# Out projection as seven products of quarter sums

## The chip, the cores and the metric

The kernel runs on one core of one Trainium2 chip, in one launch. The metric is the device time of that core in microseconds (us), median of 3 runs, 1201.58 us before the change (1201.33 to 1201.64). Engines are called as the profile calls them: PE (TensorE matmul), PEld (its weight loads), DVE (VectorE), ACT (ScalarE), POOL (GpSimd), SP (SyncE, which issues most DMAs).

## The reference

One layer: row norm, an input projection with pooling and gated linear attention, an out projection, a residual, a second row norm and a squared-ReLU MLP. What matters here is the end of the mixer and what follows it:

```python
def hybrid_mixer(u, ..., w_out):
    ...
    m = jax.nn.sigmoid(ga) * y_a + jax.nn.sigmoid(gb) * y_b
    return jnp.einsum('bld,de->ble', m, w_out)          # (1024 x 1024) x (1024 x 1024)

h = h + hybrid_mixer(rmsnorm(h, norm_mix[l]), ...)
h = h + squared_relu_mlp(rmsnorm(h, norm_ffn[l]), w_ff1[l], w_ff2[l])
return rmsnorm(h, norm_final)[:, N_META:]
```

All is float32. The kernel keeps that precision by splitting each operand into a high part (rounded to the PE format) and a low part (the rest), and forming three products: high x high, high x low, low x high (`mm3`).

## The kernel before

Tokens are taken as 8 tiles of 128, in two halves of 512. Stages in time: row norms and turns of x (0 to 50 us), gates by a seven-product scheme over quarters (`Quarters`, to about 250 us), pooling and attention (to 440), the second half's y_b blocks (`yb_block(n, 1)`, to 488), the out projection (488 to 600), the first MLP product (again `Quarters`, to about 900), the second MLP product.

The order on PE is the order in which the code is written, over the whole kernel. ACT, DVE and POOL are ordered by a scheduler by its own priorities and costs, but within `start` (the first stage) all three are in written order, and around the out projection ACT and DVE are (`in_order`, `any_order`); SP is there too for the loads (`"loads"`). A DMA that POOL issues, or that any engine issues, waits on that engine's queue until what it depends on is done.

In `start`, each row tile is squared on ACT, its scale 1/rms is made from the sum (`first_rms`) by DVE for tiles 0 to 2 and by POOL for tiles 3 to 7 and the meta rows, DVE scales the row (`normed`, L680), and PE turns it. POOL's operations are the L631 to L639 group.

The gated sum m leaves the y_b blocks as high and low parts `MH`, `ML` (per token half; 8 blocks of 128 channels). The out projection `out_tile(t, ch)` makes a product for each of 8 tiles and 2 column halves `ch`, 8 blocks x 3 matmuls each, with weights `wo` rounded by `load_wo` (ACT copy, DVE subtraction). `x_again` puts x into `acc`, and DVE adds the product to it. For `ch` = 1 the row is then complete: it is stored to `h_dram`, normed (`layer_norm`), and two tiles later turned on PE by `turn_tile`, which also forms the MLP's quarter sums.

Of the kernel before, what the change touches and what calls it, by code (L numbers as in the profile page):

```python
# [15 lines left out]
P = 128  # L16
# [99 lines left out]
def kernel(  # L116
# [52 lines left out]
    pm_dram = dp.tile([2, 2, P, 4, HALF], F32, name="pm_dram")  # L169
    hf_dram = [dp.tile([NPAIR, P, HALF], F32, name=f"hf{m}_dram") for m in range(7)]  # L170
# [66 lines left out]
    def layer_norm(xt, u):  # L237

        scaled(xt, u, inv_rms(xt, u))

    def inv_rms(xt, u):
        rows = xt.shape[0]
        ss = ln_stat[ln_n[0] % 4][:rows]
        ln_n[0] += 1
        act.activation(u, xt, ACT.Square, accum_out=ss)
        return inv_sqrt(ss, 1, 1.0 / D)

# [40 lines left out]
    A11, A12, A21, A22, S2, S1, S5, S6, S7 = range(9)  # L288
# [573 lines left out]

    def gate_stage():
# [10 lines left out]
        for _ in S["gate_run"]:  # L874
            pass
# [255 lines left out]
    def early_gates():  # L1131
# [7 lines left out]
        fetch_wo(0, 0, S["raw3"])  # L1139
# [12 lines left out]
    def yb_block(n, h):  # L1152
        j = YB[h][n]

        def fn(*wbs):
# [6 lines left out]
            for e in range(2):  # L1162
# [20 lines left out]
                if h and e and n == 1:  # L1183
                    load_wo(0, 1)()
                if not h:
                    dve.tensor_tensor(gl, b, gl, ALU.mult)
                dve.tensor_tensor(gl, gl, ml, ALU.add)
# [297 lines left out]
    def merge_open():  # L1485
# [4 lines left out]
        S["wo"] = [left.push("wo0", [P, 2, KT, HALF], F32R)]  # L1490
        S["left_acc"] = left.mark()
        S["acc"] = left.push("acc", [P, 8, D], F32)
# [4 lines left out]
        fetch_wo(0, 1, S["acc"][:, 5])  # L1497
# [5 lines left out]
    def x_again(t):  # L1503
        nc.sync.dma_start(S["acc"][:, t], x[t * P : (t + 1) * P, :])

    fetched = {}

    def fetch_wo(ch, kk, at=None):

        c, rows = slice(ch * HALF, (ch + 1) * HALF), w_out[kk * 256 : (kk + 1) * 256]  # L1510
        ap = rows[:, c].rearrange("(k p) c -> p k c", p=P)
        if at is None:
            at = raw.load(ap, D)
        else:
            nc.sync.dma_start(at.rearrange("p (k c) -> p k c", k=2), ap)
        fetched[ch, kk] = at.rearrange("p (k c) -> p k c", k=2)

    def load_wo(ch, kk):
        def fn():
            if (ch, kk) not in fetched:  # L1520
                fetch_wo(ch, kk)
            wo, r = S["wo"][ch][:, :, 2 * kk : 2 * kk + 2], fetched.pop((ch, kk))
            act.activation(wo[:, 0], r, ACT.Copy)
            pending.append(lambda: dve.tensor_tensor(wo[:, 1], r, f32(wo[:, 0]), ALU.subtract))
            if ch:
                late()

        return fn

    step(one, merge_open)  # L1530
    def wo1_open():
        any_order("order")
        raw.back()
        right.pop_to(0)
        buffer("u2", 2, D)
        S["u2p"] = right.push("u2p", [P, 2, HALF], F32)
        S["rawx0"] = right.push("rawx0", [P, D], F32)
        raw.lend(S["rawx0"])
        S["right_ff"] = right.mark()
        S["wo"].append(right.push("wo1", [P, 2, KT, HALF], F32R))  # L1540


    ORDER = (0, 4, 1, 5, 2, 3, 6, 7)

    def out_tile(t, ch):
        def fn():
            half, at = t // 4, (t % 4) * P
            wo = S["wo"][ch]
            b, n = bank("mm"), ORDER.index(t)
            for j in range(2):  # L1550
                if ch and j and n > 1:
                    turn_tile(ORDER[n - 2])
                mm3(
                    b, KT // 2, lambda i: (MH[half][:, 4 * j + i, at : at + P], ML[half][:, 4 * j + i, at : at + P]),
                    lambda i: (wo[:, 0, 4 * j + i], wo[:, 1, 4 * j + i]), first=j == 0, last=j == 1,
                )
            a = S["acc"][:, t, ch * HALF : (ch + 1) * HALF]
# [360 lines left out]
```

## Time and profile before

| | us |
|---|---|
| median of 3 runs | 1201.58 |
| span of the profiled execution (its own time; what lies around it is not in the trace) | 1200.9 |
| PE busy | 1189.0 (99%) |
| DVE busy | 873.0 (73%) |
| ACT busy | 624.7 (52%) |
| POOL busy | 64.8 (5%) |
| PE share of the chain that ended last | 91% |

Busy time of PE counts overlapping matmuls once, so a busy PE says that it never lacked work, and the distance between the starts of two matmuls says what one costs. Idle time on another engine matters only where PE, or the chain, waits for it. A name such as `acc<-b_mm,acc` is output and inputs by the program's names; b_mm, b_x, b_ms are PSUM banks.

### The profile page before, as it was taken

Reading aid. Unit: us, or ns where it says so; the run is one execution under the profiler, and the core shown is the slowest. Engines: PE = TensorE matmul, PEld = TensorE weight load, DVE = VectorE, ACT = ScalarE, POOL = GpSimd, SP = SyncE. Lnnn points to the kernel's source line nnn. Section 1 sums busy time; section 2 is a strip of 40 time slices with the busy share of each in tenths; the row PEclk is TensorE's granted clock in tenths of the full one; section 3 lists DMA queues with packets and bytes.
Section 4 is the critical chain, followed back from the end, with each engine's and each line's share of the span. In section 5 each row is a group of like instructions: output and inputs, shape, how many; then the busy total and the mean of one; then the engine's idle time right before and its main releaser. Section 6 shows DMA issues by size and latency. Waiting matters only on the chain.

```text
span 1200.9 us, 18410 instructions
## 1 busy us (share of the span) xinstructions
PE 1189.0 (99%) x6810; PEld 995.0 (83%) x6810; DVE 873.0 (73%) x1436; ACT 624.7 (52%) x1120; POOL 64.8 (5%) x102
## 2 busy tenths in 40 slices
PE   9999999999999999999999999999999999999997
PEld 8888888898998887888888888888888888888885
DVE  7886677666667888637986767767675887887686
ACT  7677567745446433215654545545454444445554
POOL 2200000000103235000000000000000000000000
PEclk9999999999999999999999999999999999999999
DMA  8243433535107676821264444445389963333532
GB/s 259 36 115 116 126 92 99 156 116 161 50 20 265 196 245 196 323 69 77 88 202 132 158 149 160 148 157 164 125 283 332 330 220 97 97 97 97 167 97 88
DMA packets 143722, 183.29 MB, mean 153 GB/s; under 512 B 10328, under 2 KB 80752, under 8 KB 143120
## 3 DMA queue, kind: packets, MB, share of 16 engines
q1 hardware_dynamic: 141648, 176.55, 45.8%
q0 software_dynamic: 1824, 5.31, 1.5%
q8 instruction: 53, 0.87, 0.3%
q14 instruction: 37, 0.30, 0.1%
q10 hardware_dynamic: 160, 0.27, 0.1%
HBM read 124.41 MB, written 57.67 MB: 152 GB/s over the span
## 4 chain that ended last, share of the span: by engine, by line
PE 91%; DVE 3%; DMA 3%; ACT 1%; issue 1%; SPq 0%; POOL 0%; DVEq 0%; ACTq 0%
PE b_mm L257 10%; PE b_mm L259 10%; PE b_mm L258 10%; PE b_ms L259 10%; PE b_ms L258 10%; PE b_ms L257 10%; PE b_x L257 8%; PE b_x L258 8%; PE b_x L259 8%; PE b_sc L1278 1%; PE b_mx L257 1%; DMA ma_dram<-o 1%; PE b_mx L259 1%; PE b_mx L258 1%; DMA o<-ma_dram 1%; DMA t<-gb_dram 1%
## 5 line engine op out<-in xcount | busy, mean ns | idle before, releaser
L257 PE MATMUL b_mm<-th,w1h 128*128 128x512 f32 (+1 forms) x308 | 115.4, 375 | 0.3 <-DVE c L847 0.3
L259 PE MATMUL b_mm<-th,w1l 128*128 128x512 f32 (+1 forms) x308 | 114.2, 371 | 0.0
L258 PE MATMUL b_mm<-tl,w1h 128*128 128x512 f32 (+1 forms) x308 | 114.1, 371 | 0.0
L257 PE MATMUL b_x<-th,w1h 128*128 128x512 f32 (+1 forms) x264 | 100.2, 380 | 0.0
L258 PE MATMUL b_x<-tl,w1h 128*128 128x512 f32 (+1 forms) x264 | 100.1, 379 | 0.0
L259 PE MATMUL b_x<-th,w1l 128*128 128x512 f32 (+1 forms) x264 | 99.7, 378 | 0.0
L275 ACT ACTIVATE w1h<-raw 128x512 fp32r<-128x512 f32 x98 | 60.7, 620 | 27.9 <-PE b_ms L258 13.6
L275 ACT ACTIVATE w1h<-fs 128x512 fp32r<-128x512 f32 x78 | 49.0, 630 | 48.3 <-PE b_ms L258 34.4
L276 DVE TENSOR_TENSOR w1l<-raw,w1h 128x512 fp32r<-128x512 f32 x98 | 67.1, 686 | 8.3 <-ACT w1h L275 8.3
L257 PEld LDWEIGHTS b_mm<-th,w1h 128*128 128x128 f32 x308 | 57.8, 188 | 11.0 <-issue 0.7
L259 PEld LDWEIGHTS b_mm<-th,w1l 128*128 128x128 f32 x308 | 57.8, 188 | 10.1
L258 PEld LDWEIGHTS b_mm<-tl,w1h 128*128 128x128 f32 x308 | 57.9, 188 | 9.6
L276 DVE TENSOR_TENSOR w1l<-fs,w1h 128x512 fp32r<-128x512 f32 x78 | 53.4, 687 | 16.6 <-ACT w1h L275 16.6
L275 ACT ACTIVATE w1h<-bt 128x512 fp32r<-128x512 f32 x44 | 27.8, 632 | 66.8 <-issue 62.7
L259 PEld LDWEIGHTS b_x<-th,w1l 128*128 128x128 f32 x264 | 49.7, 188 | 9.6
L257 PEld LDWEIGHTS b_x<-th,w1h 128*128 128x128 f32 x264 | 49.6, 188 | 9.5
L258 PEld LDWEIGHTS b_x<-tl,w1h 128*128 128x128 f32 x264 | 49.6, 188 | 9.2
L1753 DVE TENSOR_TENSOR bt<-w,w 128x512 f32<-128x512 f32 x80 | 54.8, 685 | 0.6 <-DMA w<-in_w_ff_dram 0.6
L275 ACT ACTIVATE fxh<-bt 128x512 fp32r<-128x512 f32 x36 | 22.8, 632 | 55.7 <-issue 49.8
L275 ACT ACTIVATE w1h<-rawx 128x512 fp32r<-128x512 f32 x44 | 27.4, 628 | 44.6 <-PE b_x L258 18.6
L259 PE MATMUL b_ms<-wo,w1l 128*128 128x512 f32 x128 | 49.9, 390 | 0.0
L257 PE MATMUL b_ms<-wo,w1h 128*128 128x512 f32 x128 | 49.8, 389 | 0.0
(455 smaller groups left out, 3342.3 us busy)
## 6 DMA issues: line engine op xcount, KB each, us to landing
hf_dram<-h SPq DMA_DIRECT2D x112, 256.0 KB, 2.1
raw<-hf_dram SPq DMA_DIRECT2D x112, 256.0 KB, 2.6
w<-in_w_ff_dram SPq DMA_DIRECT2D x64, 256.0 KB, 4.6
raw<-in_w_in_dram SPq DMA_DIRECT2D x22, 512.0 KB, 4.6
raw<-in_w_ff_dram SPq DMA_DIRECT2D x16, 512.0 KB, 4.1
rawx<-in_w_ff_dram SPq DMA_DIRECT2D x16, 512.0 KB, 4.2
rawx<-in_w_in_dram SPq DMA_DIRECT2D x10, 512.0 KB, 4.3
xs<-in_x_dram SPq DMA_DIRECT2D x8, 512.0 KB, 4.9
```

The source lines that it names most:

```text
L257: pe.matmul(ps, ah, bh, start=first and i == 0, stop=False, skip_group_check=more)
L258: pe.matmul(ps, ah, bl, start=False, stop=False, skip_group_check=more)
L259: pe.matmul(ps, al, bh, start=False, stop=last and i == n - 1, skip_group_check=more)
L275: act.activation(hi, a, ACT.Copy)
L276: dve.tensor_tensor(lo, a, f32(hi), ALU.subtract)
L1278: pe.matmul(b[to, e, j], kk[r, s], qq[r, s], start=True, stop=True, tile_position=(e * CH, u * CH))
L1753: dve.tensor_tensor(bt, w, S["w2"][q[3:]][:, i], ALU.add if q[2] == "+" else ALU.subtract)
```

## The change

The 1024 x 1024 x 1024 out projection is done as seven products of 512 x 512 x 512 quarters in place of eight. With A the quarters of m (first index the token half, second the channel half) and B those of w_out, the products are A11 B11, A12 B21, S2 T2, S1 T1, S3 T3, S4 B22 and A22 T4, with S1 = A22 - A21, S2 = A11 + S1, S3 = A11 - A21, S4 = S2 - A12, and T1 = B11 + B12, T3 = B12 + B22, T2 = T1 + B22, T4 = T2 + B21.

- `weight_sums` makes T1 to T4 in DRAM by eight DMAs of 1 MB from POOL: a copy and an addition for each. They are written in the gate stage, one after every sixth step.
- In the y_b blocks of the first half, the plain (unsplit) quarters A11 and -A12 are stored to `plain_dram`; those of the second half stay in `sums`. S1 to S4 are made by DVE additions and by two adding DMAs from POOL, and each is split into `MH`, `ML` in place of what stood there (`token`).
- x is no longer loaded into `acc` ahead: eight DMAs from POOL add it to `acc`.
- The last four products run tile by tile (`p5`, `p3`, `p7`, `p4`, for tile t of the half), with `row`, `normed` and `turn_tile` of finished rows between. The row order is 0, 4, 1, 2, 3, 5, 6, 7. Row 7 is scaled and turned inside the MLP stage.
- The row norm there is `first_rms` (three small operations on DVE) in place of `inv_sqrt` (four).
- The MLP's `h` lies in `acc`, its two sums in `forms` and `wx`, and the loads of `c` wait for a load before them.

```diff
+    def weight_sums():
+        b11, b12, b21, b22 = quarter(0, 0), quarter(0, 1), quarter(1, 0), quarter(1, 1)
+        for n, a, b in ((T1, b11, b12), (T3, b12, b22), (T2, wt_dram[T1], b22), (T4, wt_dram[T2], b21)):
+            pool.dma_start(wt_dram[n], a)
+            yield
+            pool.dma_start(wt_dram[n], b, accum_op=ALU.add)
+            yield
...
-        for _ in S["gate_run"]:
+        sums = weight_sums()
+        for n, _ in enumerate(S["gate_run"]):
+            if n % 6 == 5:
+                next(sums, None)
+        for _ in sums:
             pass
...
+                if h and d < 4:
+                    dve.scalar_tensor_tensor(S["sr"][:, 1, d], gl, -1.0, ml, ALU.mult, ALU.subtract)
+                    continue
+                to = S["sr"][:, 0, d - 4] if h else gl
+                dve.tensor_tensor(to, gl, ml, ALU.add)
...
+                if not h:
+                    if d > 3:
+                        act.activation(ml, gl, ACT.Copy, scale=-1.0)
+                    nc.sync.dma_start(plain_dram[d // 4][:, d % 4], ml if d > 3 else gl)
...
+        weights("B21", 1)
+        total(s1, s3)
+        pool.dma_start(s3, plain_dram[0], accum_op=ALU.add)
+        product(b[0], form[0, 0], "B11", 0, last=False)
+        act.activation(p1[0], b[0], ACT.Copy)
+        token(form[1, 0], s1, 0)
...
+        total(s2, s1)
+        pool.dma_start(s4, s2, accum_op=ALU.add)
...
+        for t in range(4):
+            m = bank("ms")
+            product(m, form[0, 0], "T2", t)
+            dve.tensor_tensor(acc[:, 4 + t, left_of], p1[t], m, ALU.subtract)
+            for r in (t, 4 + t):
+                act.activation(acc[:, r, right_of], acc[:, 4 + t, left_of], ACT.Copy, scale=-1.0)
+                pool.dma_start(acc[:, r], x[r * P : (r + 1) * P, :], accum_op=ALU.add)
+            if t < 2:
+                weights("B22", t)
...
+        def p5(t):
+            held[t] = bank("mm")
+            product(held[t], form[1, 0], "T1", t, last=False)
+            less(4 + t, held[t])
+            c, (hi, lo) = slice(t * P, (t + 1) * P), form[1, 0]
+            act.activation(hi[:, :, c], s3[:, :, c], ACT.Copy)
+            dve.tensor_tensor(lo[:, :, c], s3[:, :, c], f32(hi[:, :, c]), ALU.subtract)
+
+        def p3(t):
+            b = held.pop(t)
+            product(b, form[0, 1], "B22", t, first=False)
+            less(t, b)
+            row(t)
...
+        p5(0)
+        weights("T4", 0)
+        p3(0)
+        weights("T4", 1)
+        first_blocks()
+        p7(0)
+        normed(0)
+        p4(0)
+        turn_tile(0)
+        p5(1)
+        normed(4)
+        p3(1)
+        turn_tile(4, later=later)
...
```

Where the DMAs of `weight_sums` stand is set by the scheduler. On POOL, at the start of the program, before the change (lrraw is a small weight, wgu a constant, small the row statistics):

```order
L671 DMA lrraw_158<-in_w_in_dram 128x8x16
L562 MEMSET wgu_104 80x256
L631 ISA
L631 TENSOR_SCALAR small_99<-small_99 128x1 [waits DVE_49,Activation_49]
L636 TENSOR_TENSOR small_99<-small_99 128x1 [waits DVE_49,Activation_49,Pool_49]
```

and after it, with wt0 to wt3 for T1 to T4 and in brackets the semaphores that an instruction waits for (DMASW are those of POOL's own DMAs):

```order
L662 DMA lrraw_164<-in_w_in_dram 128x8x16
L863 DMA wt0_dram_77<-in_w_out_dram 512x512
L863 DMA wt2_dram_79<-in_w_out_dram 512x512
L553 MEMSET wgu_110 80x256
L865 DMA wt0_dram_77<-in_w_out_dram 512x512 [waits DMASW1_49]
L865 DMA wt2_dram_79<-in_w_out_dram 512x512 [waits DMASW2_49]
L863 DMA wt1_dram_78<-wt0_dram_77 16x16384 [waits DMASW3_49]
L865 DMA wt1_dram_78<-in_w_out_dram 512x512 [waits DMASW5_49]
L863 DMA wt3_dram_80<-wt1_dram_78 16x16384 [waits DMASW6_49]
L865 DMA wt3_dram_80<-in_w_out_dram 512x512 [waits DMASW7_49,DMASW0_49]
L622 ISA
L622 TENSOR_SCALAR small_105<-small_105 128x1 [waits DVE_49,Activation_49]
```

All eight now stand in front of the first row norm that POOL makes (that of row tile 3), each behind the landing that it needs.

On DVE, in the second half of the out projection, around one row: before (a tile's evacuation, the row's small operations, its scaling, the low parts of a turned row),

```order
L1559 TENSOR_TENSOR acc<-b_mm,acc 128x512
L222 TENSOR_SCALAR small<-small 128x1
L225 SCALAR_TENSOR_TENSOR small<-small 128x1
L229 TENSOR_SCALAR small<-small 128x1
L230 TENSOR_TENSOR small<-small 128x1
L249 SCALAR_TENSOR_TENSOR u_5067<-acc,small,gB 128x1024
L1586 TENSOR_TENSOR acc<-b_ms,acc 128x512
L1589 TENSOR_TENSOR tl_144<-b_ms,th_140 128x4x128
```

and after it:

```order
L1652 TENSOR_TENSOR acc<-acc,b_mm 128x512
L1669 TENSOR_TENSOR tl_150<-sums,th_146 128x4x128
L622 TENSOR_SCALAR small<-small 128x1
L624 SCALAR_TENSOR_TENSOR small<-small 128x1
L625 SCALAR_TENSOR_TENSOR small<-small 128x1
L240 SCALAR_TENSOR_TENSOR u_5100<-acc,small,gB 128x1024
L1652 TENSOR_TENSOR acc<-acc,b_mm 128x512
L215 TENSOR_TENSOR tl_142<-b_ms,th_138 128x4x128 x2
```

A row now has two evacuations (L1652) and a low part of S3 (L1669) around its norm, where it had one evacuation.

More of the change, by code (lines that the diff above doesn't have):

```diff
@@ L1501, in load_gB @@
         nc.sync.dma_start(gB, bcast(norm_ffn))
[L1503 to L1516, printed above, removed]
@@ L1518, in load_wo @@
-    def load_wo(ch, kk):
-        def fn():
[L1520 to L1526, printed above, removed]
-        return fn
+    fetched, slot = {}, {}
+    SOURCES = {
+        "B11": quarter(0, 0), "B21": quarter(1, 0), "B22": quarter(1, 1),
+        "T1": wt_dram[T1], "T2": wt_dram[T2], "T3": wt_dram[T3], "T4": wt_dram[T4],
+    }
@@ new lines, in out_projection, with product, weights, token @@
+        left_of, right_of = halves()
+        def product(b, f, name, t, first=True, last=True):
+            c, (wh, wl) = slice(t * P, (t + 1) * P), slot[name]
+            mm3(
+                b, 4, lambda i: (f[0][:, i, c], f[1][:, i, c]), lambda i: (wh[:, i], wl[:, i]),
+                first=first, last=last, more=not (first and last),
+            )
+        def weights(name, q):
+            rounded(name, q, True)()
+        def token(to, src, q):
+            k = slice(2 * q, 2 * q + 2)
+            act.activation(to[0][:, k], src[:, k], ACT.Copy)
+            dve.tensor_tensor(to[1][:, k], src[:, k], f32(to[0][:, k]), ALU.subtract)
```

247 lines of the change are left out of this document (163 added, 84 removed).

## The prediction

> **What bounds the kernel now.** I read four views in this order: the first page, the table of stages, the timelines of the stages that the change touches, and the first 50 us of GpSimd (POOL). The first page says who is busy and who is on the chain that ends last.
>
> ```profile
> span 1200.9 us, 18410 instructions
> ...
> PE 1189.0 (99%) x6810; PEld 995.0 (83%) x6810; DVE 873.0 (73%) x1436; ACT 624.7 (52%) x1120; POOL 64.8 (5%) x102
> ...
> PE 91%; DVE 3%; DMA 3%; ACT 1%; issue 1%; SPq 0%; POOL 0%; DVEq 0%; ACTq 0%
> ```
>
> TensorE is busy 99% of the span and carries 91% of the chain, so the kernel is bound by the number of its matmuls. That holds for the whole; what decides here are two stages, the first 50 us and 488 to 600 us, shown in the table of stages (columns: stage, its length, then busy us and instructions of PE, weight loads, DVE, ACT, POOL, then clock, busy share of the DMA engines, GB/s).
>
> ```profile
> 2.40:10.00 7.60, 7.39 (x49) 6.83 (x48) 3.24 (x11) 4.74 (x12) 0.28 (x1) 1.00 1.01 341
> 10.00:16.00 6.00, 5.22 (x39) 4.65 (x36) 5.83 (x12) 5.90 (x12) 0.10 (x1) 1.00 1.06 374
> ...
> 25.00:33.00 8.00, 8.00 (x68) 8.00 (x67) 7.52 (x12) 7.10 (x22) 3.36 (x13) 1.00 0.40 80
> ...
> 440.00:488.00 48.00, 47.14 (x293) 37.92 (x292) 38.80 (x58) 18.27 (x28) 24.15 (x28) 1.00 0.69 222
> 488.00:540.00 52.00, 51.95 (x230) 42.70 (x229) 21.22 (x30) 11.26 (x16) 0.00 (x0) 1.00 0.52 184
> 540.00:583.00 43.00, 43.00 (x216) 36.04 (x215) 33.26 (x68) 25.40 (x55) 0.00 (x0) 1.00 0.21 83
> 583.00:600.00 17.00, 17.00 (x84) 14.00 (x82) 16.25 (x30) 11.78 (x23) 0.00 (x0) 1.00 0.27 91
> 600.00:620.00 20.00, 19.98 (x88) 16.42 (x88) 18.67 (x32) 10.61 (x19) 0.00 (x0) 1.00 0.67 209
> ```
>
> The out projection runs without a gap on PE from 488 to 600. DVE is half idle in its first half, 77% busy from 540 and 96% from 583. In the first 16 us the DMA engines are full (1.01 and 1.06).
>
> **Term 1, the matmuls saved.** The weight's tile shows how many matmuls the projection has (first and last of its six groups), and the timeline of PE how far apart they start.
>
> ```profile
> L257 PE MATMUL b_mm<-wo,th x64: 388/389/476, 488.5 to 580.7; 128*128 128x512 f32 x64
> ...
> L259 PE MATMUL b_x<-wo,tl x64: 389/389/398, 494.8 to 574.8; 128*128 128x512 f32 x64
> ...
> 489.88 0.39 PE L257 MATMUL b_mm<-wo,th 128*128 128x512 f32 x1
> ...
> 491.92 0.39 PE L257 MATMUL b_mm<-wo,th 128*128 128x512 f32 x1
> ```
>
> Six groups of 64 are 384 matmuls. The duration of 389 ns is not their price, since they overlap: nine starts lie between 489.88 and 491.92, so one costs 2.04 / 9 = 0.227 us. Seven products of 4 tiles x 4 blocks x 3 parts are 336. The 48 that go are worth 48 x 0.227 = **-10.9 us**, all of it on the path. The eight turns (64 transposes) stay.
>
> **Term 2, the weight sums ahead of the row norms.** The eight DMAs that add up the quarters of w_out are written into the gate stage, but on POOL they stand in front of the first row norm (the order of POOL above). Five of them wait for a landing, and POOL passes nothing while it waits. What stands behind is this, in the timelines of POOL, DVE and PE:
>
> ```profile
> 1.30 1.05 POOL L671 DMA_DIRECT2D lrraw<-in_w_in_dram  x1 [0.47 <-issue]
> ...
> 15.90 0.19 POOL L631 TENSOR_SCALAR small<-small 128x1 f32<-128x1 f32 x1 [13.22 <-ACT us L626]
> ...
> 18.11 0.19 POOL L639 TENSOR_TENSOR small<-small 128x1 f32<-128x1 f32 x1
> ...
> 18.34 0.75 DVE L680 TENSOR_SCALAR us<-xs,small 128x1024 f32<-128x1024 f32 x1 [0.39 <-POOL small L639]
> ...
> 19.81 1.03 PE L598 MATMUL b_ms<-ident,us 128*128 128x128 f32 x8
> ```
>
> Today POOL is idle until 15.90, makes the scale of row tile 3 with five small operations by 18.30, DVE waits 0.39 us for it and scales the row, and PE turns it. ACT, DVE and PE run this stage in a written order, so all of them stop there if POOL is late, and from 25 us on PE has no gap in which to catch up. The delay is therefore the time at which POOL is through, less 18.3.
>
> What a landing costs, from the only DMAs that POOL issues (landing rows of the loads from pm_dram, of the copy L310 and of the addition L311, and their timeline):
>
> ```profile
> DMA to landing us min/median/max: 5.5/8.3/12.3
> ...
> DMA to landing us min/median/max: 3.3/4.0/4.7
> ...
> DMA to landing us min/median/max: 4.7/4.7/4.8
> ...
> 33.69 0.86 POOL L310 DMA_DIRECT2D fs<-in_w_in_dram  x1
> 37.30 1.32 POOL L311 DMA_DIRECT2D fs<-in_w_in_dram  x1 [2.75 <-DMA fs<-in_w_in_dram]
> ...
> 43.10 1.29 POOL L311 DMA_DIRECT2D fs<-in_w_in_dram  x1 [3.70 <-DMA fs<-in_w_in_dram]
> ```
>
> The last three rows show the mechanism: the addition L311 sits on POOL until the copy before it has landed. A copy of 1 MB lands in 5.5 us at best, 8.3 in company, 12.3 at worst. An addition of 256 KB takes 4.7 where a copy of 256 KB takes 3.3, 1.4 us more; for 1 MB that is between 5.5 (no dearer than a copy) and 5.5 + 4 x 1.4 = 11.1. The pieces here are 2 KB rows, not 512 bytes, so I take the middle, 8.3. The part of a DMA that occupies the engines is its landing less 2.7 us (1.05 MB at 374 GB/s is 2.8 of the 5.5).
>
> The chain, from 2.35 (end of the issue at 1.30): T1's copy meets full DMA engines, +8.3 = 10.7. T1's addition queues behind T3's copy (2.8), +11.1 = 21.8. T2's copy reads T1's sum and queues behind T3's addition (8.3 - 2.7 = 5.6), +11.1 = 32.9. T2's addition +8.3 = 41.2. T4's copy +5.5 = 46.7. Issue of T4's addition 1.3, five small operations 2.4: 50.4. Less 18.3 that is **+32 us**. The lower end is five copies in company with nobody, 2.35 + 27.5 + 3.7 - 18.3 = +15; the upper end, with 12.3, 13.9, 16.7, 11.1 and 8.3, is +50.
>
> Beside it: T1's and T3's copies take bandwidth from the loads of x at 2 to 16 us, which are full already; these loads come late, but inside the wait, so they cost nothing more. If that cover is gone (a short chain), they would cost up to 2.1 MB / 374 GB/s = 5.6 us.
>
> After such a wait PE starts cold. The row of the blank matmuls at the start shows that:
>
> ```profile
> 1.05 5.50 PE L691 MATMUL b_x<-fs 128*128 128x128 f32 x28 [1.05 <-DVE metab L1242]
> ...
> 6.82 0.94 PE L691 MATMUL b_x<-fs 128*128 128x128 f32 x6
> ```
>
> The first 28 took 0.196 us each, the next six 0.157; 28 x 0.04 = **+1 us**. The Trainium skill (TensorE: Matmul & The Clock Gate, Part 1) says that an idle TensorE falls to half its clock and needs about 3.4 us of work to come back; by that the loss would be about 1.7 us, an estimate, and the sum 0.7 us longer. The row agrees in kind.
>
> **Term 3, new work on DVE in the projection.** Prices by form, in ns: a 128x1024 subtraction, a 128x512 evacuation, the square of a row on ACT and its scaling on DVE.
>
> ```profile
> L1524 DVE TENSOR_TENSOR wo<-acc,wo x3: 1218/1219/1226, 484.6 to 491.8; 128x1024 fp32r<-128x1024 f32 x3
> ...
> L1559 DVE TENSOR_TENSOR acc<-b_mm,acc x8: 684/692/692, 498.5 to 581.6; 128x512 f32<-128x512 f32 x8
> ...
> L245 ACT ACTIVATE u<-acc x8: 1046/1061/1062, 538.7 to 582.6; 128x1024 f32<-128x1024 f32 x8
> ...
> L249 DVE SCALAR_TENSOR_TENSOR u<-acc,small,gB x8: 1283/1285/1287, 541.1 to 585.0; 128x1024 f32<-128x1024 f32 x8
> ```
>
> First half (three products, 144 x 0.227 = 32.7 us on PE): nineteen 128x1024 operations (weights 9, token forms 6, sums 4) x 1.22 = 23.2, four evacuations x 0.69 = 2.8, together 26 of 32.7. It fits. Second half (four products and the turns, as long on PE as now): eight more evacuations, four low parts of s3, two of T4: 12 x 0.69 + 2.4 = 10.7 us, less one small operation per row, which I leave out. DVE had 33.26 + 16.25 = 49.5 of 60 us there, and would have 60.2. In an order written out by hand that leaves waits: nothing at best, if the first half and the next stage (18.67 of 20) take it up, all 10.7 us at worst. I take **+4 us**, nearer to nothing, because the share of DVE that PE waits for is only the row chain: a row is turned two products (24 x 0.227 = 5.4 us) after it is complete, and its chain is 0.69 + 1.06 + 1.28 = 3.0 us and a few small operations on free engines. It fits unless DVE is behind.
>
> **At nothing:** SP gets 13 more rows of issues, covered by its idle queue. ACT gets four weight halves, s3, and negations, covered by 540:583's 25.40 of 43. The plain rows stored and fetched (4 MB) and half of the sums fetched (2 MB) fall in 440:520, at 222 GB/s now against 374 seen; late gate rows there would show as DVE waits of 1 to 2 us, which I leave in the 4. The additions of x (eight of 512 KB on POOL) have the time of a product each. Keeping h in acc, and the wait put on the loads of c, move nothing that PE waits for now.
>
> **Sum.** Span 1200.9 - 10.9 + 32 + 1 + 4 = 1227.0; the three runs lie at 1201.33 to 1201.64, 0.7 above the span, so 1227.7. I say **1227**.
>
> **Rivals.**
> (a) The chain is only as long as undisturbed copies: +15 in place of +32, 1210. For it: after 25 us the DMA engines are 40% busy, and a copy from DRAM in 64 KB pieces may run at full rate. Against it: additions were never seen at a copy's price. The Trainium skill (DMA: Bandwidth & Descriptors, Anatomy of one DMA) has a rule for it: such a DMA takes 2.0 us plus its bytes at 436 GB/s, 4.4 us for 1 MB, whether copy or addition; five of these would give a delay of 9.8 us, an estimate, and about 1205. The 5.5 of the trace for a first copy is already above that.
> (b) Other side: the sums land before POOL is wanted, and the matmuls decide. The place is POOL at 15.90; it holds if the five landings take 12.2 us, 2.4 each, and it decides the sign up to a delay of 5.9 us, 3.6 each. Then 1201.6 - 10.9 + 4 = 1195. Against it: even a copy of 256 KB took 3.3 us, and the engines are full at that time.
> (c) The second half goes DVE-bound, or the additions of x (5.6 us of engine time per MB, 22 us in all, behind 11 us of s3 and s4) hold back the first subtractions: term 3 at 10.7 to 18 in place of 4, 1234 to 1242.
>
> **Chances.** The forecast (1215 to 1232) 0.55; (a) 1203 to 1215 0.18; (b) below 1199 0.10; (c) or the chain's upper end, above 1232, 0.14; between 1199.2 and 1204 (0.2%, about what the measurement tells apart, is 2.4 us) 0.03. The range reaches below (a), to a chain in which each step costs what 256 KB of addition did, 4.7 (delay 11.2, and term 3 at nothing: 1203), and up to (c)'s high end: 1203 to 1242. Faster 0.10, same 0.04, slower 0.86.
>
> **What the profile after would show.** PE idle from about 20 to 50 us, with POOL as the releaser of DVE at the scaling of row tile 3; POOL waiting for wt_dram five times. The projection from its first product to its last turn 11 us shorter but for waits on DVE. I am wrong if POOL's first small operation starts before 24 us, or if the sums stand elsewhere in time.

## The result, and the profile after

The changed kernel takes **1288.32 us** (median of 4, 1287.26 to 1290.09) against 1201.49: a ratio of 1.072 (95% interval 1.071 to 1.074), 86.8 us slower. The direction was forecast; the time lies 61 us above the forecast and 46 us above the upper end of its range.

The page of the changed kernel:

```profile
span 1286.5 us, 18440 instructions
PE 1202.5 (93%) x6762; PEld 1002.0 (78%) x6762; DVE 892.3 (69%) x1448; ACT 645.9 (50%) x1152; POOL 79.3 (6%) x120
PEclk8599999999999999998789999999999999999999
```

The 48 matmuls are gone (6810 became 6762), yet PE's busy time rose by 13.5 us: the clock row dips in slices 1 and 2 and again in 19 to 21 (of 32 us each), the start and the projection.

The span grew by 85.6 us. Markers of the two traces place it: POOL is through with row tile 3's scale at 57.88 in place of 18.30 (+39.6); the first load of `kq`, late in the gate stage, and the first y_b matmul are each 41.2 us later; the last y_b matmul is 44.7 later; the first matmul on `t4h`, in the MLP, is 85.4 later, and from there on nothing is lost or gained. So the start lost **41.2**, the y_b stage (from the first y_b matmul to the last) **3.5**, the projection **40.7**. About 1.3 us more lie around the span (1288.6 for the profiled execution, 2.1 above its span; before 0.7).

POOL at the start, in its timeline:

```profile
2.36 1.33 POOL L863 DMA_DIRECT2D wt_dram<-in_w_out_dram  x2
...
12.85 1.07 POOL L865 DMA_DIRECT2D wt_dram<-in_w_out_dram  x1 [8.85 <-DMA wt_dram<-in_w_out_dram]
17.46 1.02 POOL L865 DMA_DIRECT2D wt_dram<-in_w_out_dram  x1 [3.54 <-DMA wt_dram<-in_w_out_dram]
29.25 0.52 POOL L863 DMA_DIRECT2D wt_dram<-wt_dram  x1 [10.77 <-DMA wt_dram<-in_w_out_dram]
38.00 1.01 POOL L865 DMA_DIRECT2D wt_dram<-in_w_out_dram  x1 [8.23 <-DMA wt_dram<-wt_dram]
49.67 0.52 POOL L863 DMA_DIRECT2D wt_dram<-wt_dram  x1 [10.65 <-DMA wt_dram<-in_w_out_dram]
55.41 1.01 POOL L865 DMA_DIRECT2D wt_dram<-in_w_out_dram  x1 [5.22 <-DMA wt_dram<-wt_dram]
56.55 0.19 POOL L622 TENSOR_SCALAR small<-small 128x1 f32<-128x1 f32 x1
```

POOL sits on a DMA until the one that it needs has landed, six times in all, and makes its first small operation at 56.55 in place of 15.90. DVE waits for it, and PE for DVE (timelines of the two):

```profile
57.92 0.75 DVE L671 TENSOR_SCALAR us<-xs,small 128x1024 f32<-128x1024 f32 x1 [33.34 <-POOL small L630]
```

```profile
58.82 1.94 PE b_ms L589 x8
```

(The second row is from the chain of waits; before the change eight such transposes took 1.03 us.)

The projection, as one window from its first matmul to the first on `t4h` (columns as in the table of stages), before and after:

```profile
488.70:605.30 116.60, 116.53 (x544) 96.39 (x544) 75.03 (x133) 51.04 (x98) 0.00 (x0) 1.00 0.35 126
```

```profile
533.40:690.70 157.30, 124.05 (x496) 98.68 (x496) 97.44 (x147) 70.32 (x127) 8.68 (x10) 0.87 0.50 145
```

DVE has 22 us more to do, but is busy for only 97 of 157 us; PE stands for 33 us and runs at a mean clock of 0.87. Where PE stands shows its timeline (two of nine waits over 1.5 us; the bracket is the idle time and its releaser):

```profile
575.19 0.76 PE L248 MATMUL b_mm<-w1h,th 128*128 128x512 f32 x1 [4.61 <-ACT th L1668]
575.75 0.63 PE L249 MATMUL b_mm<-w1l,th 128*128 128x512 f32 x1
576.18 0.63 PE L250 MATMUL b_mm<-w1h,tl 128*128 128x512 f32 x1
...
580.33 0.40 PE L249 MATMUL b_x<-ww,th 128*128 128x512 f32 x1
580.56 0.39 PE L250 MATMUL b_x<-ww,tl 128*128 128x512 f32 x1
...
599.69 0.79 PE L248 MATMUL b_mm<-w1h,th 128*128 128x512 f32 x1 [5.82 <-DVE acc L1652]
```

Behind such a wait the matmuls start 0.43 us apart (575.75 to 576.18) and not 0.23 (580.33 to 580.56). That is the second price of a wait. It is told below as slowed clock: the length of the projection, from the last y_b matmul to the first on `t4h` (117.0 before), less 106.1 (117.0 - 10.9 of matmuls saved), less the waits in brackets. For the changed kernel that is 157.7 - 106.1 - 33.3 = 18.3 us. It is a remainder, so whatever else lengthened the stage is in it; the distances of the starts above 0.23 us, added up over PE's timeline, give 19.5.

| kernel | time (us) | ratio to before, 95% | projection | PE waits | slowed clock |
|---|---|---|---|---|---|
| before | 1201.5 | 1 | 117.0 | 0 | 0 (with 48 matmuls more) |
| after | 1288.3 | 1.071 to 1.074 | 157.7 | 33.3 | 18.3 |
| before, with the sums alone | 1241.8 | 1.031 to 1.035 | 117.0 | 0 | 0 |
| the same, copies for additions | 1233.6 | 1.025 to 1.029 | 116.7 | 0 | 0 |
| A: after, sums behind the start | 1245.7 | 1.035 to 1.038 | 156.7 | 34.8 | 15.8 |
| A, own banks | 1238.2 | 1.028 to 1.032 | 146.4 | 28.4 | 11.9 |
| A, no x | 1240.8 | 1.031 to 1.034 | 152.3 | 27.5 | 18.7 |
| B: A, transposes later | 1226.8 | 1.019 to 1.023 | 136.7 | 20.8 | 9.8 |
| B, own banks | 1231.5 | 1.023 to 1.026 | 139.3 | 24.7 | 8.5 |
| B, own banks, no x | 1220.8 | 1.013 to 1.018 | 130.7 | 16.7 | 7.9 |
| B, x spread | 1224.1 | 1.017 to 1.020 | 136.3 | 19.0 | 11.2 |
| B, splits on POOL | 1232.4 | 1.025 to 1.028 | 145.0 | 25.7 | 13.2 |
| B, both of these | 1230.1 | 1.021 to 1.025 | 141.0 | 24.7 | 10.2 |
| C: B, norms first | 1225.1 | 1.018 to 1.022 | 135.5 | 19.2 | 10.2 |
| D: C, x spread | 1216.9 | 1.011 to 1.015 | 127.8 | 15.5 | 6.2 |
| E: D, last norm first | 1215.5 | 1.010 to 1.014 | 125.2 | 11.6 | 7.5 |
| E, forms last | 1216.2 | 1.010 to 1.013 | 124.3 | 11.8 | 6.4 |

### The profile page after: what moved, and what is told of

The parts are those of the page before. It is cut to its first block, busy times and chain, and to the rows that moved or that the text cites. A ratio compares the mean times of both kernels' runs of the same rounds, so it can differ in the third digit from the quotient of the medians.

```text
span 1286.5 us, 18440 instructions
## 1 busy us (share of the span) xinstructions
PE 1202.5 (93%) x6762; PEld 1002.0 (78%) x6762; DVE 892.3 (69%) x1448; ACT 645.9 (50%) x1152; POOL 79.3 (6%) x120
## 4 chain that ended last, share of the span: by engine, by line
PE 81%; DMA 9%; DVE 4%; ACT 3%; issue 2%; POOL 0%; SPq 0%; POOLq 0%; DVEq 0%; ACTq 0%
PE b_mm L248 10%; PE b_mm L250 9%; PE b_mm L249 9%; PE b_ms L249 9%; PE b_ms L250 9%; PE b_ms L248 9%; PE b_x L248 7%; PE b_x L249 7%; PE b_x L250 7%; DMA wt_dram<-in_w_out_dram 3%; DMA h_dram<-acc 1%; PE b_sc L1296 1%; DMA t<-gb_dram 1%; DMA wt_dram<-wt_dram 1%; PE b_mx L248 1%
## 5 line engine op out<-in xcount | busy, mean ns | idle before, releaser
L1854 ACT ACTIVATE acc<-acc 128x512 f32<-128x512 f32 x48 | 30.3, 632 | 36.9 <-DVE acc L1852 36.9
L267 DVE TENSOR_TENSOR w1l<-bt,w1h 128x512 fp32r<-128x512 f32 x44 | 30.4, 691 | 21.5 <-ACT w1h L266 21.5
```

Of the source, the lines that this page charges most:

```text
L267: dve.tensor_tensor(lo, a, f32(hi), ALU.subtract)
L1854: act.activation(h[w], b, ACT.Relu)
```

## The experiments

**The sums alone.** To the kernel before, `weight_sums` and its call in `gate_stage` are added as in the diff above; nothing else.

> The kernel before, to which only the eight weight-sum DMAs are added at the place where the changed kernel has them; nothing reads the sums. Theory: the start loses what the changed kernel lost there, because POOL issues the additions ahead of the norms of rows 3 to 8 and each waits for the DMA it adds onto: +39 to +42 us, 1240 to 1243, all of it before the gate products. Rival: part of the 41.2 us came from what else the change does to the start (row tile 7's load, the order of the gate quarters): then +15 to +35.

Measured 1241.77, +39.7 to the kernel before on the same chip; POOL's first small operation starts at 55.66, and the projection is the old one:

```profile
527.90:644.50 116.60, 116.55 (x545) 96.50 (x545) 75.06 (x132) 50.99 (x98) 0.00 (x0) 1.00 0.35 126
```

So the eight DMAs alone cost the start 39.5 of the 41.2 us, by the first load of `kq`. Of the other 1.7 us, 0.9 are POOL coming free at 56.55 in place of 55.66, and the rest is not placed.

**Copies for additions**, in the same kernel: `pool.dma_start(wt_dram[n], b)` without `accum_op`.

> The kernel before with the eight DMAs of the weight sums at the start, as in the run of the sums alone, but each addition is replaced by a plain copy of the same quarter (the four results are then no sums; nothing reads them). The order on POOL and the waits stay. Theory: half of the 40 us is the additions' own slowness (an addition of 1 MB takes 11.2 to 11.7 us in a chain where a copy takes 5.2 to 8.2): the chain then has six copies, POOL comes free 8 to 14 us sooner, and the time is 1226 to 1234. Rival: the chain's steps are set by the DMA engines, which are full from 0 to 50 us whatever kind the transfer is: within 4 us of the run of the sums alone, 1238 to 1243.

Measured 1233.62, 8.1 less by the medians of two executions each (1231.69 and 1235.54 here). The time is just inside the theory's range, but POOL did not come free 8 us sooner or more, as the theory had it. Its POOL timeline, from the slower of the two executions:

```profile
12.85 0.62 POOL L875 DMA_DIRECT2D wt_dram<-in_w_out_dram  x1 [8.89 <-DMA wt_dram<-in_w_out_dram]
...
33.64 0.63 POOL L875 DMA_DIRECT2D wt_dram<-in_w_out_dram  x1 [7.85 <-DMA wt_dram<-wt_dram]
42.95 0.50 POOL L873 DMA_DIRECT2D wt_dram<-wt_dram  x1 [8.68 <-DMA wt_dram<-in_w_out_dram]
...
49.55 0.19 POOL L632 TENSOR_SCALAR small<-small 128x1 f32<-128x1 f32 x1
```

From 33.64 to 42.95 are 9.3 us, where the addition took 11.7 in the changed kernel (38.00 to 49.67) and 12.0 in the sums alone. POOL comes free 6.1 us sooner than with additions (49.55 for 55.66), and the profiled execution is 6.2 us shorter than that of the sums alone. The chain's length, five landings behind each other, is the cost; the adding is about a sixth of it (6.1 of 39.7), and not the half that the theory had.

**A: the sums behind the start.** In the changed kernel:

```diff
-            pool.tensor_copy(mask, mf)
+            S["masked"] = pool.tensor_copy(mask, mf)
...
-        sums = weight_sums()
+        sums, behind = weight_sums(), lambda: tc.issue_after(S["masked"].ins)
         for n, _ in enumerate(S["gate_run"]):
-            if n % 6 == 5:
-                next(sums, None)
...
+            with behind():
+                next(sums if n % 6 == 5 else iter(()), None)
```

> The changed kernel, with the eight weight-sum DMAs behind POOL's last instruction of the start. Theory: the start comes back whole, the projection stays as it is: 1288.3 - 41.2 = 1247, and 1244 to 1250 if the sums now take DMA time from the gate stage's weights. Rival: the sums, now beside the gate stage's loads, hold back those loads, whose bound is DMA there: 1255 to 1280. In both the projection still takes 155 to 160 us from its first matmul to the first square of the feed-forward, so the kernel is still slower than before.

Measured 1245.74, 42.6 less. The first load of `kq` stands at 221.2 (221.3 before): in this execution the start is whole, and the gate stage loses nothing beside the sums. The projection stays at 156.7. Everything below rests on A.

The gate stage is not always as whole. The sums are now in flight from 44 to 105 us, and in the profiled executions of five versions below (B with own banks, the same without x, B with x spread, both, and E with forms last) PE waits there, by 0.8 to 2.6 us between 83 and 107 us. With own banks, on DVE and PE:

```profile
82.47 0.69 DVE L330 TENSOR_TENSOR fs<-raw 128x512 f32<-128x512 f32 x1 [4.64 <-DMA raw<-in_w_in_dram]
```

```profile
83.82 0.79 PE L250 MATMUL b_ms<-P7h,w1l 128*128 128x512 f32 x1 [2.35 <-DVE w1l L267]
```

The first load of `kq` then comes 1.8 to 4.4 us later than in A. No edit below touches this stage. That the sums delay the gate stage's loads, as the rival had it, is likely but not shown: A and B have the same sums and no such wait. So a difference of up to 4 us between two times below need not be the edit's, and the column of the projection is the safer one.

**A with own banks**: the third and fourth products get a bank each.

```diff
-            product(held[t], form[1, 0], "T1", t, last=False)
-            less(4 + t, held[t])
+            product(held[t], form[1, 0], "T1", t)
+            less(4 + t, held[t]); less(t, held[t])
...
-            b = held.pop(t)
-            product(b, form[0, 1], "B22", t, first=False)
+            b = bank("mm")
+            product(b, form[0, 1], "B22", t)
```

(the seventh and fourth products alike, in bank `x`)

> As the one before (sums after the start), and the third and fourth products each have a PSUM bank of their own, instead of adding onto the fifth and seventh in theirs; DVE takes eight more additions of 128x512 out of PSUM (8 x 0.69 = 5.5 us). PE then doesn't wait for DVE to read the partial sum before the next product. Theory A (the shared bank is the cause): the waits of PE on DVE in front of those products (4.6, 2.7, 5.8, 3.1, 1.9, 4.2, 1.7 and 4.3 us, 28 in all) go, and about 15 us of slowed clock behind them: 25 to 45 us less than the run with sums after the start, 1205 to 1222. Theory B (DVE and ACT, working through one written order and handing each row to and fro, set the pace, and the bank only shows where PE meets it): PE waits elsewhere, at the transposes or at the next bank, and the time is within 8 us of that run, or longer by up to 6.

Measured 1238.21, 7.5 less: inside theory B's 8. The waits went to the transposes, as B said (PE's timeline):

```profile
561.30 1.97 PE L1739 MATMUL b_ms<-ident,u 128*128 128x128 f32 x8 [10.72 <-DVE u L240]
...
612.63 1.94 PE L1739 MATMUL b_ms<-ident,u 128*128 128x128 f32 x8 [6.51 <-DVE u L240]
```

The shared bank is where PE meets DVE, not why DVE is late; theory A fell here. The bank was not free, though: the projection is 10.3 us shorter, net of the eight additions more on DVE, and the y_b stage 2.8 longer.

**A without the additions of x** (the loop's `pool.dma_start(acc[:, r], x...)` left out).

> As the run with sums after the start, without the eight additions of x (rows of h lack x, so this part of the computation is left out). Theory: x's additions occupy the DMA engines from 565 to 590 us and hold the first subtraction (PE waits 4.6 us) and the store of row tile 0 (14.9 us instead of 2.6, behind it ACT's copy and PE's 5.8 us): without them these two waits go, with their cold clock: 10 to 16 us less than that run, 1231 to 1237. Rival: the later rows wait as long as they do now (2 to 4 us each), since their waits have no DMA in them, and row 0's waits are replaced by DVE and ACT: less than 6 us gained.

Measured 1240.82, 4.9 less: the rival. PE's wait of 5.9 us at row 1's third product fell to 2.2, its wait at row 0's from 6.0 to 3.6; the later ones stayed.

**B: the transposes one product later**, on all engines: `turn_tile` of a row stands behind the next product instead of ahead of it.

```diff
         p4(0)
-        turn_tile(0)
         p5(1)
+        turn_tile(0)
         normed(4)
         p3(1)
-        turn_tile(4, later=later)
         p5(2)
+        turn_tile(4, later=later)
```

(and so on)

> The run with sums after the start, with each row tile's transposes written one product later (behind the next row's fifth or seventh product instead of ahead of it), on all engines; banks shared as in the changed kernel. Theory B (the hand-over from a row's last product through its norm to its transposes is longer than the two products that PE has meanwhile): DVE's subtraction out of the shared bank no longer stands behind the former row's splits, so the waits of 2 to 4 us at rows 1 to 3 shrink to about 1 us, and with their cold clock 15 to 25 us go: 1221 to 1231. Rival (DVE's own amount of work is the limit): 1240 to 1248, no change.

Measured 1226.76, 19.0 less, with no work taken from any engine: theory B. PE's waits fell from 34.8 to 20.8 us, and 6 us of slowed clock with them. On DVE the next product's read of the shared bank now stands ahead of the former row's splits (the high and low parts of a turned row); a row's norm still stands behind them. On PE the transposes now lie between that product and the one that adds onto its bank, so PE has them to do while DVE reads. Which of the two gave how much is not separated. The longest wait left is at the end:

```profile
601.16 1.94 PE L1739 MATMUL b_ms<-ident,u 128*128 128x128 f32 x8 [6.29 <-DVE u L240]
```

**B with own banks**, and **the same without x**:

> Own banks and the transposes one product later, together. Theory B: neither the bank nor the hand-over holds PE then, but for the wait of row 0's copy on its store (10.7 us in the run with own banks): 25 to 40 us below the run with sums after the start, 1206 to 1221. Rival (DVE's amount of work): no better than own banks alone, 1236 to 1242.

Measured 1231.46: neither. Of the 4.7 us more than B, 3.7 lie ahead of the first load of `kq` (225.2 for 221.6), in the gate stage. The projection is 2.6 us longer than B's: with the order mended, the banks and their eight additions on DVE no longer pay.

> As the one before, without the eight additions of x (left out of the computation). Theory: the additions fill the DMA engines for 20 us and hold row 0's store, and behind it PE by about 11 us and its cold clock: 9 to 14 us less than the one before, 1194 to 1210. Rival: the price of x stays at the 4.9 us that leaving it out gave in the run with sums after the start.

Measured 1220.84: 10.6 less than the one before it, as the theory had it; the range named for the time missed, since it hung on the run before. The projection is 8.6 us shorter. So here x has a price of 9 to 11 us, of which the run without x on A showed only half.

**B with x spread**, **with splits on POOL**, and **both**:

```diff
             for r in (t, 4 + t):
-                act.activation(acc[:, r, right_of], acc[:, 4 + t, left_of], ACT.Copy, scale=-1.0)
-                pool.dma_start(acc[:, r], x[r * P : (r + 1) * P, :], accum_op=ALU.add)
+                if r not in (2, 3):
+                    add_x(r, r < 5)
...
         weights("T4", 1)
+        add_x(2)
...
         p5(3)
+        for r in (5, 6, 7): add_x(r, True, False)
```

(`add_x` holds the two lines taken out; its arguments say whether the addition and the copy are made there; `add_x(3)` stands behind `turn_tile(0)`; and for the splits:)

```diff
-                dve.tensor_tensor(fl, a, f32(fh), ALU.subtract)
+                pool.tensor_tensor(fl, a, f32(fh), ALU.subtract)
```

(the low part of `t4h` in the MLP stage alike)

> As the run with transposes one product later (sums after the start, shared banks), with the additions of x spread: rows 0, 4 and 1 as soon as their rows are ready, rows 2 and 3 behind row 0's and row 4's norm, rows 5 to 7 after p5 of row 3. Theory: row 0's store no longer stands behind 4 MB of additions and the first subtraction finds its rows sooner: what leaving x out gave beside own banks (10.6 us) comes mostly back: 1215 to 1221. Rival: the additions now delay rows 1 to 7 instead: within 4 us of that run's 1226.8.

Measured 1224.07, 2.7 less: the rival. The profiled executions are alike (1226.1 and B's 1226.0). The transfers did what they should (median landings, from the issues between 505 and 600; in B, x took 11.1 and the stores 3.4, and the slowest store 15.5, here 4.9):

```profile
acc<-in_x_dram POOLq DMA_DIRECT2D x8, 512.0 KB, 5.6
h_dram<-acc SPq DMA_DIRECT2D x7, 512.0 KB, 2.6
```

but PE still waited 4.0 us for the first subtraction, that of row 4 (DVE stood there for row 4's addition of x, but only 0.8 us).

> As the run with transposes one product later; the twelve low halves of the sixth, seventh and fourth form (128x512, out of SBUF) go from DVE to POOL, which is idle there and takes 1.28 us for one where DVE takes 0.69. Theory: DVE, busy for 33.5 of the 40 us from 580 to 620, is what rows 5 to 7 wait for (2.4, 1.3, 6.3 and 0.9 us with the cold clock behind them): 8.3 us come off it, 5 to 12 us less, 1215 to 1222. Rival (the hand-over's latency and not the load): within 4 us of 1226.8.

Measured 1232.40, 5.6 **slower** (PE waits 1.9 us longer already at 533 us, ahead of POOL's first subtraction at 589). DVE lost twelve operations and its busy time in the projection rose from 96.1 to 100.9 us. Its timeline, while POOL subtracts (POOL's rows below it):

```profile
597.65 0.68 DVE L1756 TENSOR_TENSOR acc<-b_ms,acc 128x512 f32<-128x512 f32 x1
598.25 1.59 DVE L1757 TENSOR_TENSOR acc<-acc 128x512 f32<-128x512 f32 x1
...
599.83 1.69 DVE L335 TENSOR_TENSOR s<-raw,raw 128x512 f32<-128x512 f32 x1
601.44 1.21 DVE L624 SCALAR_TENSOR_TENSOR small<-small 128x1 f32<-128x1 f32 x1
```

```profile
598.02 1.27 POOL L1826 TENSOR_TENSOR t4l<-acc,t4h 128x512 fp32r<-128x512 f32 x1 [6.39 <-ACT t4h L1825]
599.25 1.72 POOL L1763 TENSOR_TENSOR forms<-acc,forms 128x512 fp32r<-128x512 f32 x1
600.93 1.71 POOL L1763 TENSOR_TENSOR wx<-acc,wx 128x512 fp32r<-128x512 f32 x1
```

L1757 and L335 take 0.68 us in B, L624 0.22. Operations with one operand in PSUM (L1756) kept their 0.68. The Trainium skill has this (SBUF — State Buffer, Who interferes with whom): a DVE instruction with two inputs in SBUF contends with a GpSimd instruction that reads SBUF. The trace agrees. So this run doesn't test the amount of work on DVE: it raised it.

> The two edits before in one kernel. If both theories hold, their gains add up, since they are in different rows: 1203 to 1214. If neither holds: within 5 us of 1226.8. Below 1201.5, the kernel before, only if the y_b stage's 2.5 us and the slowed clock go as well, which no theory here expects.

Measured 1230.13: neither; the loss of the one and the small gain of the other.

**C: norms first.** The same work, the order of ACT and DVE written anew.

```diff
         weights("T4", 0)
-        p3(0)
         weights("T4", 1)
+        p3(0)
...
         p5(1)
-        turn_tile(0)
         normed(4)
+        turn_tile(0)
...
-        turn_tile(6)
+        turn_tile(6, later=later)
+        for fn in later: fn()
```

(each row's `normed` likewise ahead of the former row's `turn_tile`; row 5's forms deferred like row 6's)

> As the run with transposes one product later, with the order on DVE and ACT written anew and no work taken away: each row's norm ahead of the former row's splits, both halves of the fourth weight converted before the third product, and the sixth and seventh forms of rows 5 and 6 behind row 7's sum. Theory B, sharpened (PE waits for a row that is ready but stands behind other rows' splits in DVE's written order): the waits at the transposes (1.7, 0.8, 0.5, 2.4, 6.3 and 0.9 us) and the 2.7 us at the fourth product go, with their cold clock: 12 to 22 us below 1226.8, 1205 to 1215. Rival (DVE's amount of work, 84 per cent busy from 580 to 620 us, or the latency of the norm itself): the waits come back at other places, within 5 us of 1226.8.

Measured 1225.14, 1.6 less: the rival. Waits at the transposes of rows 0 to 6 went, as expected; PE waited instead at row 2's third product and at row 7's transposes, whose norm now stood behind the deferred forms:

```profile
556.81 0.79 PE L248 MATMUL b_mm<-w1h,th 128*128 128x512 f32 x1 [3.92 <-DVE acc L1652]
...
604.73 1.94 PE L1740 MATMUL b_ms<-ident,u 128*128 128x128 f32 x8 [7.14 <-DVE u L240]
```

**D: C with x spread** (row 4's addition behind its first subtraction, rows 2 and 3 behind the first and second p3, rows 5 to 7 as above).

> The same, and the additions of x spread: rows 0 and 1 as before, row 4 behind its first subtraction, rows 2 and 3 behind the first and second p3, rows 5 to 7 behind p5 of row 3. Theory: the first subtraction and row 0's store then have nothing to wait for, and 4 to 6 us of PE's wait at the first third product go, with 2 of cold clock: 5 to 10 us below the run before, 1197 to 1209. Rival: the spread gives 2.7 us, as it did with the old order.

Measured 1216.93, 8.2 less than C: the step was as expected, the range not, since it hung on C. In the new order spreading x shortens the projection by 7.7 us, in the old one by 0.4. What went is the wait of 3.9 us at row 2's third product, and 4 us of slowed clock. But it is not the same spread, since row 4's addition, too, stands behind the first subtraction here, so how much is the order's is not separated.

**E: last norm first** (`normed(7)` ahead of `turn_tile(6)`, both `weights("B22", q)` ahead of the loop of the T2 products), and **E with forms last** (row 4's x behind `p7(0)`, the deferred forms behind the MLP's first evacuation).

> As the run before (new order, x spread), with two more places set in order and no work taken away: row 7's norm ahead of row 6's splits and of the four deferred forms, and both halves of the second product's weights converted ahead of the seven products' p1 - m subtractions. Theory B: PE's last wait (7.1 us at row 7's transposes) falls to about 2, and the first (3.3 us at the third product) to about 1, with some cold clock: 6 to 11 us below 1216.9, 1206 to 1211, still slower than before. Rival (DVE's amount of work, 18.4 of 20 us from 580 to 600): what row 7's norm gains the splits lose, and the feed-forward's first products wait instead: 1213 to 1218.

Measured 1215.49, 1.4 less: the rival's range. The two waits aimed at fell from 7.1 to 0.6 and from 3.3 to 0.9 us, and two others grew, one behind DVE's wait for x, one behind ACT's forms:

```profile
537.84 0.77 PE L248 MATMUL b_x<-wz,th 128*128 128x512 f32 x1 [3.92 <-DVE small L622]
...
593.13 1.06 PE L1752 MATMUL b_ms<-ident,u 128*128 128x128 f32 x8 [0.55 <-DVE u L240]
597.38 0.50 PE L248 MATMUL b_x<-th,w1h 128*128 128x512 f32 x1 [3.18 <-ACT u2p L384]
```

> The run before with two edits of order alone: row 4's addition of x behind its second subtraction instead of its first, and the sixth and seventh forms of rows 5 and 6 behind the feed-forward's first evacuation. Theory B: of the stalls left there (3.9 us at row 0's fourth product behind DVE's wait for x, 3.2 us behind ACT's forms at the feed-forward's second product, 1 us each at four more) the two long ones go, with about 2 us of cold clock: 6 to 9 us below 1215.5, 1206 to 1210, and by then the projection takes about what it took before, so that the saved 10.9 us of matmuls are just eaten by short stalls, cold clock and the 2.5 us of the y_b stage. Rival: the forms are then late for the sixth and seventh products of the feed-forward, and PE waits there as long: 1213 to 1217.

Measured 1216.18, no change: the rival (the projection is 1.0 us shorter, but the first load of `kq` comes 2.1 us later than in E). Both waits went (3.9 to 0.9, 3.2 to 1.1) and came back a little further on, at row 1's third product and at the MLP's next evacuation:

```profile
546.93 0.50 PE L248 MATMUL b_mm<-w1h,th 128*128 128x512 f32 x1 [2.76 <-DVE acc L1659]
...
602.79 0.79 PE L248 MATMUL b_x<-th,w1h 128*128 128x512 f32 x1 [2.70 <-ACT u2p L384]
```

These two edits of order gave 1.4 us and nothing. In this stretch of E, DVE is nearly full:

```profile
580.00:600.00 20.00, 15.40 (x72) 11.81 (x71) 18.31 (x33) 10.92 (x23) 0.00 (x0) 0.95 0.31 105
```

## Why the prediction was wrong

**Term 1 was right in what it counted.** The projection's window has 496 PE instructions in place of 544. None of the 10.9 us reached the end.

**Term 2: the mechanism right, the size short.** +41.2 for +33. Against the steps in the prediction: T1's copy 10.5 for 8.3, T1's addition 16.4 for 11.1 (it ran beside T3's copy and addition), T2's copy 8.7 for 11.1, T2's addition 11.7 for 8.3, T4's copy 5.7 for 5.5. The addition lies above even my upper end, 11.1, which I had from four times a difference in 256 KB. Six of the DMAs wait for a landing, not five: T3's addition waits too (3.54 us at 17.46), inside the landing of T1's addition, so the chain of five stands. Rival (a), with copies' prices, falls: with copies in fact the time was 1233.6 on the old projection. The Trainium skill's rule for one DMA (DMA: Bandwidth & Descriptors, Anatomy of one DMA), which gave about 1205, falls with it: it has one price by size, 4.4 us for 1 MB by my estimate, and none apart for additions, while in this chain the copies took 5.7 to 10.5 us and the additions 11.7 and more. For the cold start 41.2 - 39.6 leaves 1.6 us; I had 1, and the estimate from the Trainium skill (TensorE: Matmul & The Clock Gate, Part 1) was 1.7. In the sums alone the same difference is 0.8, so no run shows how much of the 1.6 is the clock's.

**Term 3 is the step that failed.** Of the 61 us, 8 are term 2's and 51 are here: projection and y_b stage together were to be 6.9 us shorter (-10.9 + 4) and were 44.2 longer. The failed sentence is that "the share of DVE that PE waits for is only the row chain". It compared that chain (3.0 us and small operations, from a row's last product to its transposes) with the two products that PE has meanwhile (5.4 us). But eight of the nine waits over 1.5 us stand in front of a third or fourth product. Such a product adds onto the bank of the product just before it, and DVE must read that bank in between. Only the ninth, 3.70 us at row 7's transposes, is at the end of a row chain. DVE was late because it and ACT work in one written order, and its read of the bank stood behind the former row's splits. Ahead of the wait of 5.82 us, DVE's timeline (L215 a split of row 0, L1652 the read):

```profile
598.35 0.69 DVE L215 TENSOR_TENSOR tl<-b_ms,th 128x512 fp32r<-128x512 f32 x1 [0.29 <-ACT th L214]
598.96 0.68 DVE L1652 TENSOR_TENSOR acc<-acc,b_mm 128x512 f32<-128x512 f32 x1
```

PE had been idle since 593.9 and went on at 599.69. Row 4's transposes, the end of a row chain, followed at 604.35 without a wait. In B the same read starts when PE's product ends, and the splits come behind it:

```profile
548.56 0.69 DVE L1652 TENSOR_TENSOR acc<-acc,b_mm 128x512 f32<-128x512 f32 x1 [2.05 <-PE b_mm L250]
...
553.23 0.69 DVE L215 TENSOR_TENSOR tl<-b_ms,th 128x512 fp32r<-128x512 f32 x1 [3.38 <-ACT th L214]
```

B shows the price: the same work, 19.0 us less with that read ahead of the splits and the transposes between the two products. C, which also put the norm ahead of the splits, gave 1.6 us more.

The clock was not in the sum here at all, and cost 18.3 us beside 33.3 of waits. By the starts in PE's timeline, the eight waits of 1.87 us and more cost 1.9 to 3.3 us each in this way, 0.43 between starts in place of 0.23, and the other three (0.23, 1.03 and 1.74 us) about 0.3. The Trainium skill (TensorE: Matmul & The Clock Gate, Part 1), which I applied at the start only, has an idle stretch of about 3.4 us slow the clock. By that the five waits above 3.4 us would cost 1.7 us each, 8.5 in all, an estimate. Here waits of 1.87, 2.68 and 3.11 us were followed by slowed matmuls too, and the measurement decides.

**"The additions of x have the time of a product each"** failed too. They cost 5 to 11 us, depending on the order around them (4.9 in A, 10.6 with own banks; 8.2 for spreading them in C), in two places, the first subtraction and row 0's store. The latter I had not seen: ACT's copy into `acc` waits until the store has read it, and that store, begun while the additions were in flight, landed after 14.9 us (median of the eight stores 2.6; in A without x the slowest took 3.9).

```profile
596.26 0.60 ACT L1744 ACTIVATE acc<-b_ms 128x512 f32<-128x512 f32 x1 [3.53 <-DMA h_dram<-acc]
```

Rival (c) named both, DVE's load and x, but priced them as work (10.7 to 18 us), not as a hand-over that repeats for every row and lets the clock fall behind most of its waits. Hence the range was too low. The y_b stage, left in the 4, cost 3.5. DVE's waits for late gate rows are there (1.9 and 2.5 us), but PE's own waits in it (2.8 us, 0.9 before) are mostly for converted weights, so what cost the 3.5 is not shown.

**The direction was right by the size of term 2.** By terms 1 and 3 alone the kernel was to be faster, and in A, without the start's loss, it is still 43.7 us slower.

**What stays open.** Three causes are shown: the written order (19.0 us), x's additions (5 to 11), and the clock behind most waits. In E, 11.6 us of waits are left, and the last two edits moved them on. DVE's share there (18.3 of 20 us) speaks for its amount of work, but the one run that was to lower it raised it, so that is argued and not shown. Also open: the gate stage's late loads beside the sums, and 1.3 us around the span. No version beat the kernel before: the best, E, is 1.0 to 1.4% slower, because 7.5 us of slowed clock, 11.6 of waits and 2.6 in the y_b stage are more than 10.9.

## What to carry to other kernels

Fewer matmuls pay only if PE's stream stays whole: count, for each hand-over (product to evacuation to norm to transpose), what stands ahead of it in the written order of each engine on the way, compare that with PE's work in between, and charge each gap of about 2 us or more twice, once as a wait and once as slowed clock (here 1.9 to 3.3 us for each of eight). A DMA that must wait for another belongs on a queue with nothing urgent behind it: moving the eight sums behind POOL's last instruction of the start gave back 42.6 us with an edit of a few lines; look then at what they meet in the stage where they run. Before work is moved from DVE to POOL, look whether DVE's own operations beside it have two operands in SBUF.

## What the hardware showed that I had not expected

- An adding DMA of 1 MB from DRAM to DRAM takes 11.7 us where a copy of the same rows took 9.3, and eight additions of 512 KB at once land after 11.1 us each (median), in 5.6 when spread.
- A wait need not be long to slow the clock, and a longer one may not. The half clock comes in stretches: in the changed kernel the granted clock is 0.50 from 572.9 to 579.7 us, 1.00 to 586.5, 0.50 to 589.9. In A's timeline of PE, 3.09 us of idling left it at full speed (the row after it 0.39 us), 2.18 us did not (0.63):

```profile
568.44 0.50 PE L248 MATMUL b_mm<-w1h,th 128*128 128x512 f32 x1 [3.09 <-DVE acc L1652]
568.78 0.39 PE L249 MATMUL b_mm<-w1l,th 128*128 128x512 f32 x1
...
577.26 0.77 PE L248 MATMUL b_mm<-w1h,th 128*128 128x512 f32 x1 [2.18 <-DVE acc L1652]
577.82 0.63 PE L249 MATMUL b_mm<-w1l,th 128*128 128x512 f32 x1
```

- While POOL subtracts out of SBUF, DVE's operations on two SBUF operands take 1.6 to 1.7 us for 0.68 at 128x512, and even 128x1 ones 1.2 for 0.22.
